# The gain row norm_g spread by TensorE instead of by a load, and the last row tile cut into 512, 384 and 128 columns

## The chip, the cores and the metric

The kernel runs on one core of one Trainium2 chip. The time is device microseconds of one execution; the figure for a kernel is the median over its runs. TensorE multiplies matrices, ScalarE (ACT in the profile), VectorE (DVE) and GpSimd (POOL) work on rows of up to 128 partitions, and SyncE (SP) issues most of the loads and stores. ScalarE can issue some as well.

## The reference, cut to what matters

One decoder block over 1,040 tokens of 1,024 features: 16 learned meta tokens stand ahead of 1,024 real ones.

```python
def rmsnorm(x, g):
    xf = x.astype(jnp.float32)
    xf = xf * lax.rsqrt(jnp.mean(xf * xf, axis=-1, keepdims=True) + RMS_EPS)
    return (xf * g.astype(jnp.float32)).astype(x.dtype)

def hybrid_layer(x, norm_g, w_in, ...):
    h = rmsnorm(x, norm_g)
    proj = jnp.einsum('bld,dn->bln', h, w_in)
    u_pool, z_pool, q, k, v, z_attn, f_logit, g_pool, g_attn = jnp.split(proj, ...)
    y_pool = causal_multiscale_pool(u_pool, pool_w, pool_scale) * jax.nn.silu(z_pool)
    y_attn = forgetting_attention(q, k, v, log_f).reshape(...) * jax.nn.silu(z_attn)
    merged = (jax.nn.sigmoid(g_pool) * jnp.einsum('blc,cd->bld', y_pool, w_up_pool)
              + jax.nn.sigmoid(g_attn) * jnp.einsum('blc,cd->bld', y_attn, w_up_attn))
    return x + jnp.einsum('bld,de->ble', merged, w_out)

h = rmsnorm(hybrid_layer(concat([meta, x]), ...), final_norm_g)[:, N_META:]
```

The change touches both ends: the first `rmsnorm` with the gain `norm_g`, and the last product with `w_out`, the residual sum and the final `rmsnorm`.

## The kernel before, in words

**Arithmetic.** Every fp32 factor is split into a high part in the fp32r format and the rest (`whi` and `wlo` of the weights, `hh` and `hl` of the normalized tokens). A product is three matmuls: high by high, low by high, high by low. A projection piece (`g_proj`, L139) has 8 blocks of 128 features and so 24 matmuls into one PSUM bank, `pj`.

**The start.** From L346 on, each engine does its work in the order in which it is written. The tokens come in nine tiles of 128 rows, `xt`. For each tile ScalarE squares it and sums the rows (`norm_scale`, L171), GpSimd adds EPS and takes the power -0.5 (`rstd_of`, L110 and L111), and VectorE multiplies the tile by that `rstd` and by the gain in one instruction (L174). For the gain it reads `gb`, the row `norm_g` in all 128 partitions; two loads of 256 KB put it there, which read the same 2 KB of the row 128 times each. TensorE then turns the scaled tile in two groups of four transposes (L185), ScalarE copies each group to `hh` (L187) and VectorE subtracts for `hl` (L188). ScalarE also makes the high part of each weight (L366). GpSimd subtracts for the low part (L371); for the q weight GpSimd takes one half and VectorE the other.

TensorE's order is: 12 warm-up matmuls on a tile of ones (`WARM`, L353, their result is not used), the transposes of tiles 0 and 1, the q piece of the first 256 tokens (the 16 meta tokens have no query, so it has 240 columns), the transposes of tile 2, the k piece, the transposes of tile 3, the v piece, and then the same for the next 256 tokens. A piece's result is copied from PSUM by ScalarE (`qa` at L211, `ka`, `vt`), so ScalarE does its later work only behind it. The v weight's high part stands on ScalarE behind the q piece's copies.

**The middle.** Sixteen units of attention, the pooling mixer, the up projections and the spilled gates follow; a filler puts projection pieces between the attention's matmuls. Their order is the same before and after the change, apart from where GpSimd's two memsets of `ql` and one mask stand in the start.

**The end.** `out_tile(i, parts)` makes one of 8 row tiles of the output. For each part of the columns TensorE does 24 matmuls (`o_mm`, L839), VectorE adds the residual row `xr` (L853), ScalarE squares and sums (L854), and VectorE multiplies by `fgb`, the gain of the final norm. GpSimd adds up the sums (L858) and takes the power (L860). Then VectorE scales the left half, ScalarE the right half (L864), and each half is stored, by SyncE's and by ScalarE's queue. The parts are two of 512 columns, and in the last row tile 512, 256 and 256.

Of the kernel before, what the change touches and what calls it, by code (L numbers as in the profile page):

```python
# [20 lines left out]
EPS = 1e-6  # L21
# [8 lines left out]
HALVES = ((0, 512), (512, 1024))  # L30
# [8 lines left out]
NRC = 2  # L39
REC0 = 2  # L40
EVAC = (((0, 1),), ((0,), (1,)))
WARM = 12


def r32(ap):
    return ap.bitcast(F32)
# [7 lines left out]
def tile_hybrid_block(ctx, tc, x, meta, norm_g, w_in, b_forget, pool_w, pool_scale,  # L54
                      w_up_pool, w_up_attn, w_out, final_g, out):
    nc = tc.nc
    x2 = x.rearrange("b s d -> (b s) d")
    o2 = out.rearrange("b s d -> (b s) d")
# [12 lines left out]
    sm = ctx.enter_context(tc.tile_pool(name="sm", bufs=2))  # L71
    dr = ctx.enter_context(tc.tile_pool(name="dr", bufs=1, space=bass.MemoryType.DRAM))
    pj = ctx.enter_context(tc.tile_pool(name="pj", bufs=PJ, space=PS))
# [8 lines left out]
    epsp = cst.tile([128, 1], F32, name="epsp")  # L82
# [24 lines left out]
    def rstd_of(ss):  # L107
        n = ss.shape[0]
        r = sm.tile([128, 1], F32, name="rstd", bufs=4)
        nc.gpsimd.tensor_scalar(r[:n], ss, EPS, None, op0=ALU.add)  # L110
        nc.gpsimd.tensor_tensor(r[:n], r[:n], epsp[:n], op=ALU.pow)  # L111
        return r

# [39 lines left out]
    ap_ = A.enter_context(tc.tile_pool(name="ap", bufs=1))  # L153

    gb = gp.tile([128, D], F32, name="gb", tag="g")
    junk = gp.tile([128, D], F32, name="junk", tag="g")

    def norm_load(i):
        c0 = i * 128
        n = min(128, L - c0)  # L160
        xt = ap_.tile([128, D], F32, name="xt", tag="s", bufs=6)
        if i == 0:
            nc.sync.dma_start(xt[NM:], x2[:128 - NM, :])
            nc.sync.dma_start(xt[:NM], meta)
        else:
            nc.sync.dma_start(xt[:n], x2[c0 - NM:c0 - NM + n, :])
        return xt

    def norm_scale(xt, n, parts=((0, D),)):
        ss = sm.tile([128, 1], F32, name="ss")  # L170
        nc.scalar.activation(junk[:n], xt[:n], AF.Square, scale=D ** -0.5, accum_out=ss[:n])  # L171
        r = rstd_of(ss[:n])
        for c0, c1 in parts:
            nc.vector.scalar_tensor_tensor(xt[:n, c0:c1], xt[:n, c0:c1], r[:n], gb[:n, c0:c1],  # L174
                                           op0=ALU.mult, op1=ALU.mult)

    def norm_t(i, xt, n):
        c0 = i * 128
# [14 lines left out]
    def rows(e):  # L193
        return slice(64 * e, 64 * e + 64), slice(64 - 64 * e, 128 - 64 * e)

    def alloc_q(p):
        for e in range(2):
            QA[p, e] = gp.tile([128, SEQ], F32R, name="qa", tag="g")
            QL[p, e] = gp.tile([128, SEQ], F32R, name="ql", tag="g")
            nc.gpsimd.memset(r32(QL[p, e])[rows(e)[1]], 0.0)  # L200

    def alloc_k(p):
        for e in range(2):
            KA[p, e] = gp.tile([128, L], F32R, name="ka", tag="g")
# [141 lines left out]
    SM.enter_context(tc.manual_schedule())  # L346
    onesr = cst.tile([128, 128], F32R, name="onesr")
    nc.vector.memset(r32(onesr), 1.0)
    nc.scalar.activation(junk[:1, :2], r32(onesr)[:1, :2], AF.Square)
    xts = {0: norm_load(0)}  # L350
    warm = psO.tile([128, 512], F32, name="po")
    for i in range(WARM):
        nc.tensor.matmul(warm, onesr, onesr[:, None, :].to_broadcast([128, 4, 128]), start=True, stop=True)  # L353
    xts[1] = norm_load(1)
    for c0, c1 in HALVES:
        nc.sync.dma_start(gb[:, c0:c1], bass.AP(tensor=norm_g.tensor, offset=norm_g.offset + c0,
                                                ap=[[0, 128], [1, c1 - c0]]))

    def load_raw(col, pool=None, tag="raw"):
        raw = (pool or wp).tile([128, KO, 128], F32, name="raw", tag=tag)  # L360
# [3 lines left out]
    def split_hi(raw, pool, tag):  # L364
        hi = pool.tile([128, KO, 128], F32R, name="whi", tag=tag)
        nc.scalar.activation(hi, raw, AF.Copy)  # L366
        return hi
# [5 lines left out]

    rq = load_raw(COL_Q)
    xts[2] = norm_load(2)
    rk = load_raw(COL_K)
    xts[3] = norm_load(3)
# [3 lines left out]
    def scale_(i):  # L381
        norm_scale(xts[i], ntok(i))

    norm_scale(xts[0], 128, HALVES)
    norm_scale(xts[1], 128, HALVES)
    alloc_q(0)
    alloc_k(0)
    norm_t(0, xts[0], 128)
    hq_ = split_hi(rq, wp, "wh")
# [3 lines left out]
    norm_t(1, xts[1], 128)  # L393
    nc.vector.tensor_tensor(lq_[:, KO // 2:], rq[:, KO // 2:], r32(hq_)[:, KO // 2:], op=ALU.subtract)
    wq = (hq_, lq_)
    norm_scale(xts[2], 128, HALVES)
    hk_ = split_hi(rk, wp, "wh")
    wk = split_lo(rk, hk_, wp, "wl")
# [4 lines left out]
    for n, (kind, t0, t1) in enumerate(todo):  # L403
# [11 lines left out]
        i = {0: 2, 1: 3, 3: 4, 4: 5, 6: 6, 7: 7, 8: 8}.get(n)  # L415
# [268 lines left out]
    def btile(name, dt=F32, tag="b"):  # L684
        return bp.tile([128, SEQ], dt, name=name, tag=tag, bufs=8 if tag == "y" else 5)
# [149 lines left out]
    def o_mm(ps, i, c0, c1, ks):  # L835
        r = slice(i * 128, (i + 1) * 128)
        for k in ks:
            for n, (a, b) in enumerate(((0, 0), (0, 1), (1, 0))):
                nc.tensor.matmul(ps[:, :c1 - c0], mg[k][a][:, r], wo[k][b][:, c0:c1], start=(k == 0 and n == 0),  # L839
                                 stop=(k == KO - 1 and n == 2))  # L840

    def out_tile(i, parts):
        r = slice(i * 128, (i + 1) * 128)
        xr = btile("xr", F32, "y")
        sq = btile("sq", F32, "y")
        nc.sync.dma_start(xr, x2[r, :])
        ss = sm.tile([128, 4], F32, name="sso")
        tot = sm.tile([128, 1], F32, name="sst")
        for n, (ps, c0, c1) in enumerate(parts):
            if ps is None:  # L850
                ps = bank()
                o_mm(ps, i, c0, c1, range(KO))
            nc.vector.tensor_tensor(xr[:, c0:c1], ps[:, :c1 - c0], xr[:, c0:c1], op=ALU.add)  # L853
            nc.scalar.activation(sq[:, c0:c1], xr[:, c0:c1], AF.Square, scale=D ** -0.5, accum_out=ss[:, n:n + 1])  # L854
            if n == 0:
                nc.gpsimd.tensor_scalar(tot, ss[:, :1], EPS, None, op0=ALU.add)
            else:
                nc.gpsimd.tensor_tensor(tot, tot, ss[:, n:n + 1], op=ALU.add)  # L858
            nc.vector.tensor_tensor(xr[:, c0:c1], xr[:, c0:c1], fgb[:, c0:c1], op=ALU.mult)
        nc.gpsimd.tensor_tensor(tot, tot, epsp, op=ALU.pow)  # L860
        (a0, a1), (b0, b1) = HALVES
        nc.vector.tensor_scalar(sq[:, a0:a1], xr[:, a0:a1], tot, None, op0=ALU.mult)
        nc.sync.dma_start(o2[r, a0:a1], sq[:, a0:a1])
        nc.scalar.activation(sq[:, b0:b1], xr[:, b0:b1], AF.Copy, scale=tot)  # L864
        nc.scalar.dma_start(o2[r, b0:b1], sq[:, b0:b1])

    first = [(i, c0, c1, bank()) for i in range(3) for c0, c1 in HALVES]
    for i, c0, c1, ps in first:
# [3 lines left out]
    for i in range(3):  # L872
        out_tile(i, [(ps, c0, c1) for i2, c0, c1, ps in first if i2 == i])
    for i in range(3, 8):
        parts = HALVES if i < 7 else ((0, 512), (512, 768), (768, 1024))
        out_tile(i, [(None, c0, c1) for c0, c1 in parts])


# [26 lines left out]
```

## Time and profile before

| | |
|---|---|
| median of 3 runs | 799.68 us (799.35 to 800.86) |
| the profiled execution | 797.71 us, of which 796.0 us are the span of the core |
| mean granted TensorE clock of it | 0.984 of full speed |
| TensorE matmuls busy | 768.6 us, 97% of the span |
| TensorE weight loads busy (they overlap the matmuls) | 655.2 us, 82% |
| VectorE busy | 469.1 us, 59% |
| ScalarE busy | 394.6 us, 50% |
| GpSimd busy | 302.8 us, 38% |

The span is the time from the first to the last instruction that the profile records; the execution's own time lies 1.7 us above it. Busy is an average over the whole span. The profiled execution is one of many, and lies 1.97 us below the median of the timed runs.

### The profile page before, as it was taken

What the parts mean: (1) busy time and instruction counts of PE and PEld (TensorE: products, weight loads), DVE (VectorE), ACT (ScalarE), POOL (GpSimd) and SP (SyncE); (2) the same over time, 40 slices, a digit from 0 to 9 for tenths busy, and PEclk for the clock granted to TensorE, in tenths of its full rate; (3) what the DMA queues carried; (4) which work ended last, traced back from release to release, by engine and by line L of the source; (5) the groups of instructions that cost most, each with busy time, mean ns of one, the idle gap of its engine ahead of it and who ended that gap; (6) DMA issues with size and microseconds to landing.
All of it is one profiled execution on the core that took longest, in us unless ns stands there. A gap on an engine that the chain in (4) does not pass through costs nothing.

```text
span 796.0 us, 10676 instructions
## 1 busy us (share of the span) xinstructions
PE 768.6 (97%) x3893; PEld 655.2 (82%) x3893; DVE 469.1 (59%) x767; ACT 394.6 (50%) x754; POOL 302.8 (38%) x243
## 2 busy tenths in 40 slices
PE   7999999999999999999998899999997999999996
PEld 6997899998898888898977778888884888888885
DVE  4843667557677575586699894571246456444232
ACT  5752466446576564575455554463335445232121
POOL 5520226325325343254262362262887122222111
PEclk7999999999999999999998999999998999999999
DMA  9311122221311312212305333335753555533331
GB/s 296 83 28 27 52 65 71 78 76 40 94 41 48 91 47 75 80 34 68 105 1 153 106 101 100 99 92 165 219 180 106 177 181 171 185 106 106 105 107 53
DMA packets 74116, 79.86 MB, mean 100 GB/s; under 512 B 5552, under 2 KB 56752, under 8 KB 74064
## 3 DMA queue, kind: packets, MB, share of 16 engines
q1 hardware_dynamic: 68096, 59.79, 24.7%
q10 hardware_dynamic: 5968, 19.40, 7.8%
q8 instruction: 30, 0.49, 0.3%
q14 instruction: 22, 0.18, 0.1%
HBM read 58.10 MB, written 21.07 MB: 99 GB/s over the span
## 4 chain that ended last, share of the span: by engine, by line
PE 85%; DVE 8%; issue 2%; DMA 2%; ACT 1%; POOL 1%; SPq 0%; POOLq 0%; DVEq 0%; ACTq 0%
PE pj L139 62%; PE pj L839 11%; PE po L590 4%; PE ps L525 2%; PE ps L524 2%; DVE s L752 1%; DVE pl L574 1%; DMA u<-sp_u 1%; PE pj L445 1%; DVE m L540 1%; DVE u L756 1%; DMA gb<-in_norm_g_dram 1%; PE pt L553 1%; DVE S L569 1%; PE pt L545 1%
## 5 line engine op out<-in xcount | busy, mean ns | idle before, releaser
L139 PE MATMUL pj<-hh,whi 128*128 128x512 f32 (+4 forms) x768 | 183.0, 365 | 1.4 <-DVE ql L215 0.9
L139 PE MATMUL pj<-hh,wlo 128*128 128x512 f32 (+4 forms) x768 | 183.2, 363 | 0.0
L128 POOL TENSOR_TENSOR wlo<-raw,whi 128x1024 fp32r<-128x1024 f32 x37 | 91.3, 2469 | 239.0 <-ACT whi L127 81.9
L139 PE MATMUL pj<-hl,whi 128*128 128x512 f32 (+4 forms) x768 | 178.1, 361 | 0.0
L139 PEld LDWEIGHTS pj<-hh,whi 128*128 128x128 f32 x768 | 132.7, 191 | 19.2 <-PE pj L249 1.1
L139 PEld LDWEIGHTS pj<-hh,wlo 128*128 128x128 f32 x768 | 133.1, 191 | 16.8
L139 PEld LDWEIGHTS pj<-hl,whi 128*128 128x128 f32 x768 | 132.3, 190 | 17.4 <-DVE hl L188 0.2
L574 DVE TENSOR_TENSOR pl<-S,ph 128x512 fp32r<-128x512 f32 (+4 forms) x112 | 84.4, 765 | 15.7 <-ACT ph L573 14.8
L582 POOL TENSOR_TENSOR acc<-acc,S 128x272 f32<-128x272 f32 (+4 forms) x80 | 79.0, 988 | 19.4 <-ACT S L570 10.4
L533 ACT ACTIVATE S<-ps,negc 128x400 f32<-128x400 f32 (+2 forms) x96 | 49.0, 515 | 55.9 <-DVE S L531 49.9
L540 DVE TENSOR_TENSOR m<-m,S 128x272 f32<-128x272 f32 (+4 forms) x80 | 55.1, 689 | 18.1 <-ACT S L533 16.7
L569 DVE TENSOR_TENSOR S<-S,pt 128x512 f32<-128x512 f32 (+4 forms) x112 | 50.2, 499 | 17.8 <-PE pt L553 17.7
L573 ACT ACTIVATE ph<-S 128x512 fp32r<-128x512 f32 (+4 forms) x112 | 52.5, 479 | 11.8 <-PE po L590 11.3
L570 ACT ACTIVATE S<-S 128x512 f32<-128x512 f32 (+4 forms) x112 | 48.1, 477 | 16.2 <-DVE S L569 16.1
L839 PE MATMUL pj<-wol,gh 128*128 128x512 f32 (+1 forms) x136 | 51.7, 380 | 0.0
L839 PE MATMUL pj<-woh,gl 128*128 128x512 f32 (+1 forms) x136 | 51.7, 380 | 0.0
L839 PE MATMUL pj<-woh,gh 128*128 128x512 f32 (+1 forms) x136 | 51.6, 379 | 0.0
L819 POOL TENSOR_TENSOR gl<-rl,gh 128x512 fp32r<-128x512 f32 x16 | 22.6, 1412 | 72.5 <-ACT gh L818 72.4
L127 ACT ACTIVATE whi<-raw 128x1024 fp32r<-128x1024 f32 x37 | 39.1, 1056 | 17.8 <-PE pj L139 17.6
L815 DVE TENSOR_TENSOR rl<-pj,rl 128x512 f32<-128x512 f32 x32 | 22.0, 690 | 40.1 <-PE pj L139 36.7
L287 ACT ACTIVATE st<-pj 128x512 f32<-128x512 f32 x48 | 28.5, 593 | 32.7 <-PE pj L139 23.4
L590 PE MATMUL po<-pl,V 128*128 128x512 f32 (+4 forms) x112 | 38.1, 340 | 2.8 <-DVE pl L574 2.8
(166 smaller groups left out, 1163.1 us busy)
## 6 DMA issues: line engine op xcount, KB each, us to landing
raw<-in_w_in_dram SPq DMA_DIRECT2D x40, 512.0 KB, 3.9
sp_gp<-st SPq DMA_DIRECT2D x16, 256.0 KB, 2.3
sp_ga<-st SPq DMA_DIRECT2D x16, 256.0 KB, 4.0
rl<-sp_gp ACTq DMA_DIRECT2D x8, 512.0 KB, 3.8
rl<-sp_ga ACTq DMA_DIRECT2D x8, 512.0 KB, 3.7
rawo<-in_w_out_dram SPq DMA_DIRECT2D x8, 512.0 KB, 4.0
xr<-in_x_dram SPq DMA_DIRECT2D x8, 512.0 KB, 3.8
xt<-in_x_dram SPq DMA_DIRECT2D x7, 512.0 KB, 9.4
```

The source lines that it names most:

```text
L127: nc.scalar.activation(hi, raw, AF.Copy)
L128: (eng or nc.gpsimd).tensor_tensor(lo, raw, r32(hi), op=ALU.subtract)
L139: nc.tensor.matmul(ps, a, b, start=(i == 0), stop=(i == len(seq) - 1))
L533: nc.scalar.activation(s[:kb, f0:], ps[:kb, f0:], AF.Identity, bias=nb_)
L540: nc.vector.tensor_tensor(m[:kb, c0:], m[:kb, c0:], s[:kb, c0:], op=ALU.max)
L569: dves.append(nc.vector.tensor_tensor(s[:kb, c0:], s[:kb, c0:], self.pm[:kb, c0:], op=ALU.subtract))
L570: exps.append(nc.scalar.activation(s[:kb, c0:], s[:kb, c0:], AF.Exp))
L573: nc.scalar.activation(ph[:kb, c0:], s[:kb, c0:], AF.Copy)
L574: nc.vector.tensor_tensor(pl[:kb, c0:], s[:kb, c0:], r32(ph[:kb, c0:]), op=ALU.subtract)
L582: nc.gpsimd.tensor_tensor(acc[:kb, c0:], acc[:kb, c0:], s[:kb, c0:], op=ALU.add)
L590: nc.tensor.matmul(self.po[:, c0:], v, r[:kb, c0:], start=(b == 0 and i == 0), stop=(b == self.nb - 1 and i == 1))
L839: nc.tensor.matmul(ps[:, :c1 - c0], mg[k][a][:, r], wo[k][b][:, c0:c1], start=(k == 0 and n == 0), stop=(k == KO - 1 and n == 2))
```

## The change

At the start, `norm_g` comes as one row of 4 KB into one partition, by ScalarE's queue. Two matmuls, with a row of ones as the stationary side, put the row into 128 partitions of two PSUM banks. They stand behind four warm-up matmuls, one more follows, and the other seven go. The scaling of tiles 0 and 1 reads the gain from PSUM. Behind tile 1, ScalarE copies both banks to `gb` for the later tiles. The 16 meta rows are loaded by ScalarE's queue instead of SyncE's, and VectorE adds EPS instead of GpSimd. GpSimd's memsets of `ql` come later.

At the end, the last row tile is cut at 512 and 896 instead of 512 and 768. In all row tiles the last of the sums is added by VectorE, with one instruction of one column, instead of GpSimd. In the last one VectorE scales and stores 640 columns and ScalarE 384.

```diff
@@ constants
-WARM = 12
+WARM = (4, 1)
+LAST = ((0, 512), (512, 896), (896, 1024))
@@ rstd_of
-        nc.gpsimd.tensor_scalar(r[:n], ss, EPS, None, op0=ALU.add)
+        nc.vector.tensor_scalar(r[:n], ss, EPS, None, op0=ALU.add)
@@ norm_load, tile 0
-            nc.sync.dma_start(xt[:NM], meta)
+            nc.scalar.dma_start(xt[:NM], meta)
@@ norm_scale
-            nc.vector.scalar_tensor_tensor(xt[:n, c0:c1], xt[:n, c0:c1], r[:n], gb[:n, c0:c1],
-                                           op0=ALU.mult, op1=ALU.mult)
+            g = gps[c0 // 512][:n] if gps else gb[:n, c0:c1]
+            nc.vector.scalar_tensor_tensor(xt[:n, c0:c1], xt[:n, c0:c1], r[:n], g, op0=ALU.mult, op1=ALU.mult)
@@ the start
+    grow = ap_.tile([1, D], F32, name="grow")
+    nc.scalar.dma_start(grow, norm_g)
...
+    warm_up(WARM[0])
+    gps = []
     for c0, c1 in HALVES:
-        nc.sync.dma_start(gb[:, c0:c1], bass.AP(tensor=norm_g.tensor, offset=norm_g.offset + c0,
-                                                ap=[[0, 128], [1, c1 - c0]]))
+        pg = pj.tile([128, 512], F32, name="pj")
+        nc.tensor.matmul(pg, r32(onesr)[:1], grow[:, c0:c1], start=True, stop=True)
+        gps.append(pg)
+    warm_up(WARM[1])
@@ behind norm_t(1) and the halves of the q weight's low part
+    for g, (c0, c1) in zip(gps, HALVES):
+        nc.scalar.activation(gb[:, c0:c1], g, AF.Copy)
+    gps.clear()
+    alloc_q(0)
     norm_scale(xts[2], 128, HALVES)
@@ out_tile
+            elif n < len(parts) - 1:
+                nc.gpsimd.tensor_tensor(tot[:, :1], tot[:, :1], ss[:, n:n + 1], op=ALU.add)
             else:
-                nc.gpsimd.tensor_tensor(tot, tot, ss[:, n:n + 1], op=ALU.add)
+                nc.vector.tensor_scalar(tot[:, 1:], ss[:, n:n + 1], tot[:, :1], None, op0=ALU.add)
+                nc.gpsimd.tensor_tensor(tot[:, 1:], tot[:, 1:], epsp, op=ALU.pow)
...
-        (a0, a1), (b0, b1) = HALVES
...
+        (a0, a1), (b0, b1) = HALVES if i < 7 else ((0, 640), (640, 1024))
```

ScalarE's order from the start of the program to the square of tile 2 was this before (`xt` is a token tile, `hh_115` and `hh_116` the two halves of `hh`, `whi` a weight's high part, `junk` a result that is not used):

```order
L349 ACT_TABLE_LOAD
L349 ACTIVATE junk<-onesr 1x2
L171 ACTIVATE junk,ss<-xt 128x1024 x2
L187 ACTIVATE hh_115<-pt 128x4x128
L187 ACTIVATE hh_116<-ps 128x4x128
L366 ACTIVATE whi<-raw 128x1024
L187 ACTIVATE hh_115<-pt 128x4x128
L187 ACTIVATE hh_116<-ps 128x4x128
L171 ACTIVATE junk,ss<-xt 128x1024
```

After the change the same stretch reads:

```order
L351 DMA grow<-in_norm_g_dram 1x1024
L165 DMA xt<-in_meta_tokens_dram 16x1024
L353 ACT_TABLE_LOAD
L353 ACTIVATE junk<-onesr 1x2
L172 ACTIVATE junk,ss<-xt 128x1024 x2
L188 ACTIVATE hh_115<-pt 128x4x128
L188 ACTIVATE hh_116<-ps 128x4x128
L376 ACTIVATE whi<-raw 128x1024
L188 ACTIVATE hh_115<-pt 128x4x128
L188 ACTIVATE hh_116<-ps 128x4x128
L406 ACTIVATE gb<-pj 128x512 x2
L172 ACTIVATE junk,ss<-xt 128x1024
```

Two loads are issued ahead of all work, and the two copies of `gb` from PSUM stand between the copies of tile 1 and the square of tile 2, with the splits and the later squares behind them.

VectorE's order from the scaling of tile 0 to that of tile 3 was this before (`hl` is the low part of the tokens, `wlo` the half of the q weight's low part):

```order
L174 SCALAR_TENSOR_TENSOR xt<-xt,rstd,gb 128x512 x4
L188 TENSOR_TENSOR hl_117<-pt,hh_115 128x4x128
L188 TENSOR_TENSOR hl_118<-ps,hh_116 128x4x128
L188 TENSOR_TENSOR hl_117<-pt,hh_115 128x4x128
L188 TENSOR_TENSOR hl_118<-ps,hh_116 128x4x128
L394 TENSOR_TENSOR wlo<-raw,whi 128x512
L174 SCALAR_TENSOR_TENSOR xt<-xt,rstd,gb 128x512 x2
L174 SCALAR_TENSOR_TENSOR xt<-xt,rstd,gb 128x1024
```

After the change the same stretch, to the EPS of tile 3, reads:

```order
L111 TENSOR_SCALAR rstd<-ss 128x1
L176 SCALAR_TENSOR_TENSOR xt<-xt,rstd,pj 128x512 x2
L111 TENSOR_SCALAR rstd<-ss 128x1
L176 SCALAR_TENSOR_TENSOR xt<-xt,rstd,pj 128x512 x2
L189 TENSOR_TENSOR hl_117<-pt,hh_115 128x4x128
L189 TENSOR_TENSOR hl_118<-ps,hh_116 128x4x128
L189 TENSOR_TENSOR hl_117<-pt,hh_115 128x4x128
L189 TENSOR_TENSOR hl_118<-ps,hh_116 128x4x128
L403 TENSOR_TENSOR wlo<-raw,whi 128x512
L111 TENSOR_SCALAR rstd<-ss 128x1
L176 SCALAR_TENSOR_TENSOR xt<-xt,rstd,gb 128x512 x2
L111 TENSOR_SCALAR rstd<-ss 128x1
```

The adds of EPS to the row sums stand between the scalings, so that of tile 1 comes behind both halves of tile 0. Tiles 0 and 1 are scaled by the PSUM banks `pj`, tile 2 and the later ones by `gb`.

## Rows read from the trace of the kernel before

**Rows 1.** Chain of waits, first 32 us (start us, us, what).
```profile
2.17 6.66 DMA gb<-in_norm_g_dram
...
13.85 5.43 PE pj L139 x24
20.76 2.82 PE pj L139 x24
24.46 6.02 PE pj L139 x48
```

**Rows 2.** Windows: stretch, us, busy of PE, PEld, DVE, ACT, POOL; granted clock, DMA, GB/s.
```profile
9.00:19.00 10.00, 8.83 (x40) 8.43 (x40) 8.39 (x10) 6.13 (x10) 7.64 (x8) 0.50 1.09 361
19.10:25.00 5.90, 5.66 (x48) 5.32 (x47) 4.18 (x7) 5.60 (x12) 4.24 (x5) 1.00 1.00 260
```

**Rows 3.** Timeline of the start (start us, us, what [idle before, released by]).
```profile
1.31 4.92 PE L353 MATMUL po<-onesr 128*128 128x512 f32 x12 [1.31 <-DVE car L477]
...
4.77 1.06 ACT L171 ACTIVATE junk<-xt 128x1024 f32<-128x1024 f32 x1 [2.48 <-DMA xt<-in_meta_tokens_dram]
...
6.46 0.57 POOL L111 TENSOR_TENSOR rstd<-rstd,epsp 128x1 f32<-128x1 f32 x1
...
7.54 1.06 ACT L171 ACTIVATE junk<-xt 128x1024 f32<-128x1024 f32 x1 [1.62 <-DMA xt<-in_x_dram]
...
8.95 2.74 DVE L174 SCALAR_TENSOR_TENSOR xt<-xt,rstd,gb 128x512 f32<-128x512 f32 x4 [7.68 <-DMA gb<-in_norm_g_dram]
...
9.76 1.12 PE L185 MATMUL pt<-ident,xt 128*128 128x128 f32 x4 [3.53 <-DVE xt L174]
```

**Rows 4.** Timeline of ScalarE, 13 to 22 us.
```profile
13.68 0.60 ACT L187 ACTIVATE hh<-ps 128x512 fp32r<-128x512 f32 x1
14.16 1.07 ACT L171 ACTIVATE junk<-xt 128x1024 f32<-128x1024 f32 x1
...
19.30 1.49 ACT L211 ACTIVATE qa<-pj 64x240 fp32r<-64x240 f32 x4 [2.01 <-PE pj L139]
20.70 1.05 ACT L366 ACTIVATE whi<-raw 128x1024 fp32r<-128x1024 f32 x1
```

**Rows 5.** Timelines of VectorE and GpSimd, 16 to 25 us.
```profile
16.41 2.37 POOL L371 TENSOR_TENSOR wlo<-raw,whi 128x1024 fp32r<-128x1024 f32 x1
16.48 3.51 DVE L174 SCALAR_TENSOR_TENSOR xt<-xt,rstd,gb 128x512 f32<-128x512 f32 x2 [0.77 <-POOL rstd L111]
...
19.49 0.93 POOL L111 TENSOR_TENSOR rstd<-rstd,epsp 128x1 f32<-128x1 f32 x1
...
20.45 1.29 DVE L174 SCALAR_TENSOR_TENSOR xt<-xt,rstd,gb 128x1024 f32<-128x1024 f32 x1 [0.47 <-POOL rstd L111]
...
21.83 2.42 POOL L371 TENSOR_TENSOR wlo<-raw,whi 128x1024 fp32r<-128x1024 f32 x1 [1.41 <-ACT whi L366]
```

**Rows 6.** Timeline of TensorE: the last 48 matmuls, the first and the last.
```profile
783.73 0.28 PE L839 MATMUL pj<-woh,gh 128*128 128x256 f32 x1
...
789.25 0.28 PE L839 MATMUL pj<-woh,gl 128*128 128x256 f32 x1
```

**Rows 7.** Timeline of TensorE's weight loads, 143.2 to 143.6 us.
```profile
143.28 0.19 PEld L139 LDWEIGHTS pj<-hh,wlo 128*128 128x128 f32 x1
...
143.39 0.19 PEld L590 LDWEIGHTS po<-ph,V 128*128 128x128 f32 x1
```

**Rows 8.** Timelines of VectorE, ScalarE and GpSimd after the last matmul.
```profile
789.57 0.42 DVE L853 TENSOR_TENSOR xr<-pj,xr 128x256 f32<-128x256 f32 x1 [1.39 <-PE pj L839]
...
790.03 0.42 ACT L854 ACTIVATE sq<-xr 128x256 f32<-128x256 f32 x1 [2.31 <-DVE xr L853]
...
790.68 0.36 POOL L858 TENSOR_TENSOR sst<-sst,sso 128x1 f32<-128x1 f32 x1 [2.45 <-ACT sq L854]
791.12 0.57 POOL L860 TENSOR_TENSOR sst<-sst,epsp 128x1 f32<-128x1 f32 x1
...
791.72 0.72 ACT L864 ACTIVATE sq<-xr,sst 128x512 f32<-128x512 f32 x1 [1.19 <-POOL sst L860]
```

More of the change, by code (lines that the diff above doesn't have):

```diff
@@ L348, in tile_hybrid_block, with warm_up @@
     nc.vector.memset(r32(onesr), 1.0)
+    grow = ap_.tile([1, D], F32, name="grow")
+    nc.scalar.dma_start(grow, norm_g)
+    xts = {0: norm_load(0)}
     nc.scalar.activation(junk[:1, :2], r32(onesr)[:1, :2], AF.Square)
-    xts = {0: norm_load(0)}
+    xts[1] = norm_load(1)
     warm = psO.tile([128, 512], F32, name="po")
-    for i in range(WARM):
-        nc.tensor.matmul(warm, onesr, onesr[:, None, :].to_broadcast([128, 4, 128]), start=True, stop=True)
-    xts[1] = norm_load(1)
+    def warm_up(n):
+        for i in range(n):
+            nc.tensor.matmul(warm, onesr, onesr[:, None, :].to_broadcast([128, 4, 128]), start=True, stop=True)
+    warm_up(WARM[0])
+    gps = []
     for c0, c1 in HALVES:
-        nc.sync.dma_start(gb[:, c0:c1], bass.AP(tensor=norm_g.tensor, offset=norm_g.offset + c0,
-                                                ap=[[0, 128], [1, c1 - c0]]))
+        pg = pj.tile([128, 512], F32, name="pj")
+        nc.tensor.matmul(pg, r32(onesr)[:1], grow[:, c0:c1], start=True, stop=True)
+        gps.append(pg)
+    warm_up(WARM[1])
     def load_raw(col, pool=None, tag="raw"):
@@ L385, in tile_hybrid_block @@
     norm_scale(xts[1], 128, HALVES)
-    alloc_q(0)
     alloc_k(0)
@@ L847, in out_tile @@
         ss = sm.tile([128, 4], F32, name="sso")
-        tot = sm.tile([128, 1], F32, name="sst")
+        tot = sm.tile([128, 2], F32, name="sst")
         for n, (ps, c0, c1) in enumerate(parts):
@@ L855, in out_tile @@
             if n == 0:
-                nc.gpsimd.tensor_scalar(tot, ss[:, :1], EPS, None, op0=ALU.add)
-            else:
-                nc.gpsimd.tensor_tensor(tot, tot, ss[:, n:n + 1], op=ALU.add)
+                nc.gpsimd.tensor_scalar(tot[:, :1], ss[:, :1], EPS, None, op0=ALU.add)
+            elif n < len(parts) - 1:
+                nc.gpsimd.tensor_tensor(tot[:, :1], tot[:, :1], ss[:, n:n + 1], op=ALU.add)
+            else:
+                nc.vector.tensor_scalar(tot[:, 1:], ss[:, n:n + 1], tot[:, :1], None, op0=ALU.add)
+                nc.gpsimd.tensor_tensor(tot[:, 1:], tot[:, 1:], epsp, op=ALU.pow)
             nc.vector.tensor_tensor(xr[:, c0:c1], xr[:, c0:c1], fgb[:, c0:c1], op=ALU.mult)
-        nc.gpsimd.tensor_tensor(tot, tot, epsp, op=ALU.pow)
-        (a0, a1), (b0, b1) = HALVES
-        nc.vector.tensor_scalar(sq[:, a0:a1], xr[:, a0:a1], tot, None, op0=ALU.mult)
+        (a0, a1), (b0, b1) = HALVES if i < 7 else ((0, 640), (640, 1024))
+        nc.scalar.activation(sq[:, b0:b1], xr[:, b0:b1], AF.Copy, scale=tot[:, 1:])
+        nc.scalar.dma_start(o2[r, b0:b1], sq[:, b0:b1])
+        nc.vector.tensor_scalar(sq[:, a0:a1], xr[:, a0:a1], tot[:, 1:], None, op0=ALU.mult)
         nc.sync.dma_start(o2[r, a0:a1], sq[:, a0:a1])
-        nc.scalar.activation(sq[:, b0:b1], xr[:, b0:b1], AF.Copy, scale=tot)
-        nc.scalar.dma_start(o2[r, b0:b1], sq[:, b0:b1])
     first = [(i, c0, c1, bank()) for i in range(3) for c0, c1 in HALVES]
@@ L874, in tile_hybrid_block @@
     for i in range(3, 8):
-        parts = HALVES if i < 7 else ((0, 512), (512, 768), (768, 1024))
+        parts = HALVES if i < 7 else LAST
         out_tile(i, [(None, c0, c1) for c0, c1 in parts])
```

## The prediction

> **What bounds the kernel now.** I read the chain of waits first, over the first 25 us: the reader is to see that it does not begin with arithmetic but with a load, the 128-fold copy of norm_g, from 2.17 to 8.83, and that TensorE then carries it: the q piece of 24 matmuls from 13.85 to 19.28, the k piece from 20.76 to 23.58 [rows 1]. Then the windows with the granted clock: 0.50 from 9 to 19 us, that is 1.2 GHz, and 1.00 (2.4 GHz) from 19.1 on [rows 2], so the clock rises just before the k piece. Then the timeline of the start [rows 3], of ScalarE [rows 4], and of VectorE against GpSimd [rows 5], because the places between those two TensorE stretches are set there. Last the tail [rows 6 to 8]. Order is the same in between, so what is gained by the v piece, and what is lost on the last row tile, is all that the change can do directly.
>
> **The change part by part: the start.**
>
> *The load.* The scaling of row tile 0 sat idle for norm_g until 8.95, although its rstd was done at 6.46 + 0.57 = 7.03 [rows 3]. With the load gone, the scaling starts at about 7.0: 1.9 us earlier. (The add of EPS moves from GpSimd to VectorE; that may give some tenths more, and I count nothing.)
>
> *Is the spread there in time?* Four warm-up matmuls end at 1.31 + 4 x 0.41 = 2.95 (12 of them take 4.92) [rows 3]. The 4 KB row is issued at about the time of the first x load, and that load and the meta rows, 512 KB in all, had landed at 4.77 [rows 3]; the row lands no later. No matmul of this kind is in the trace: a pass of 512 columns costs 0.41 as in the warm-up; four passes, my upper bound, 1.64. The halves are then ready at 6.4 and 8.05 at the latest, at 3.8 and 4.2 at the earliest if the row lands at 3.4. They are needed at 7.0 and 7.7. Cost: 0, at worst 0.4; I take 0, the work of tile 0's square and rstd covers it.
>
> *Tile 1.* Its square is released by its own load at 7.54 [rows 3], which I leave there. 7.54 + 1.06, the read of the sum (about 0.2), the add, now on VectorE behind tile 0's scalings, and 0.57 for the power give 9.6; it was 8.95 + 2 x 0.69 = 10.3. One half scaled (0.69), four transposes at half clock (1.12) and one ScalarE copy (0.60) [rows 3, 4] put the q piece at about 12.0 instead of 13.85: 1.85 earlier.
>
> *The copies of gb.* Two ScalarE copies of 128x512 from PSUM come between tile 1's copies and the square of tile 2. The step from such a copy to the next instruction is 14.16 - 13.68 = 0.48 [rows 4], so 0.96 in all. The square of tile 2, the split of the k weight and everything behind them on ScalarE are then earlier by 0.9 only.
>
> *Where that 0.9 goes.* The scaling of tile 2 and GpSimd's subtract for the k weight started together, at 16.48 and 16.41; the scaling took 3.51 for two halves that take 1.37 at the start (2.74 for four) [rows 3, 5]: 2.1 us lost to the 2.37 us subtract. Both hang on the same ScalarE stretch, both move by 0.9 and meet again. The k piece stands on TensorE behind tile 2's transposes, so it starts at 20.76 - 0.9 = 19.9.
>
> *The clock in the k piece.* The q piece ends by 12.0 + 5.43 = 17.4. TensorE then waits some 2 us, with four transposes in it. Before, it had worked on from 13.85 with no such pause and got the full clock at 19.1. After its other pause, from 6.23 (1.31 + 4.92) to 9.76, it stood at 1.2 GHz [rows 2, 3]. If the k piece runs at half clock it costs 2.82 more, if at full clock nothing. I take 1.0, part of the piece, nearer to the row that shows a pause followed by half clock but with a shorter pause. End of the k piece: 23.58 - 0.9 + 1.0 = 23.7.
>
> *Tile 3.* Here the earlier q piece triggers a new collision. Before, tile 3 was scaled from 20.45 to 21.74 while GpSimd stood idle until 21.83 for the split of the v weight, which ScalarE could only make at 20.70 because it had waited 2.01 us for the q piece [rows 4, 5]. With q done at 17.4 or earlier, that split ends at 19.85 or earlier; tile 3's power ends at 20.42 - 0.9 = 19.5, and GpSimd goes straight into the 2.42 us subtract, as it did at 16.41. The scaling ends at about 19.6 + 2.4 + 1.29 = 23.3 instead of 21.74. Its transposes followed the k piece at 23.58 anyway, so this loss hides behind that of the clock: the v piece follows the later of 23.7 and 23.3, against 23.58. If the clock holds, 23.3 is the bound and 0.3 is gained.
>
> Start, sum: 0.0 (-0.3 to +0.1 as worked). Bounds: -1.85 when nothing behind the q piece binds, +1.9 when the whole k piece runs at half clock.
>
> **The last row tile.** Before, the 48 matmuls of 256 columns start every (789.25 - 783.73) / 47 = 0.1175 [rows 6]. 24 of 384 columns, by columns, start every 0.176: 4.2 us. For 128 columns half of 0.1175 would be 0.059, 1.4 us, and TensorE would end when it did. But each matmul loads its own weights, and where short matmuls follow each other the loads start at 143.28 and 143.39 [rows 7], 0.11 apart: 24 x 0.11 = 2.6 us. I take that, since it is the row of the very limit: 4.2 + 2.6 - 5.6 = **+1.2** (bounds 0 and 1.2).
>
> The Trainium skill (TensorE: Matmul & The Clock Gate, Back-to-back issue gap) gives about 81 ns per matmul of 128 columns in a stream with its weight loads. By that the piece would take 24 x 0.081 = 1.9 and TensorE would end 0.5 later, not 1.2. The row of this trace is slower than that page.
>
> What follows the last matmul took 789.57 to 791.72 + 0.72 = 792.44, that is 2.87 [rows 8]. The add of 0.42 and the square of 0.42 work on half the columns: I take 0.1 off each. GpSimd's add with its hand-over, 791.12 - 790.68 = 0.44, becomes a VectorE add of one column, about 0.15: 0.3 off. The last copy has 384 instead of 512 columns: 0.72 x 0.25, 0.15 off. The read, the power (0.57) and the store stay, and VectorE's 640 columns run beside ScalarE's 384. Sum **-0.65** (-0.4 to -0.9). The last tile: +0.55, bounds -0.9 and +0.8. The same VectorE add in tiles 0 to 6 is hidden: TensorE's matmuls run on, and the add stands before a multiply that waits for the same square.
>
> **Sum.** 0.0 + 0.55 = +0.5 on the profiled execution's 797.71 (span 796.0 and 1.7 around it): 798.2. The median of the runs is 1.97 above it. I put that down to the clock: in the profiled execution it rose just as the k piece began, the best case; a run in which it rises later pays in the k piece already before the change, and the 1.0 that I charged above is then no new loss. On the median the sum is so between -0.5 and +0.5; I take -0.2: **799.5**.
>
> **The rivals.**
>
> *Faster: the start's gain survives.* If VectorE is first at tile 3, or the v weight arrives late, and the clock stays up, the k piece's 0.9 reaches the v piece; if the copies of gb do not bind either, 1.85 does. With a last tile at its lower bound of -0.9: 799.7 - 0.9 - 0.9 = 797.9, to 799.7 - 1.85 - 0.9 = 796.9. For it: the long idle time ahead of the scaling, which truly goes. Against it: the 3.51 us scaling [rows 5], which shows that VectorE does wait out GpSimd.
>
> *Slower: the pause costs the clock.* If TensorE's pause ahead of the k piece leaves it at 1.2 GHz for the whole of the k piece and part of the v piece, 2.8 to 3.3 are lost against 0.9 gained; with +0.55 at the end 799.7 + 2.5 to 3.0 = 802.2 to 802.7. It decides once more than about 4 us of matmuls run at half clock after 19.9. For it: the pause at 6.23 and the 10 us at half clock that followed. Against it: the median already holds executions with a later rise, and the transposes of tile 2 break the pause.
>
> *The change does not do what it says* (the spread is late, the scaling waits as long as before): the k piece starts where it did and the tail adds 0.55: 800.2, within my forecast's band.
>
> **How the numbers follow.** About 0.2%, 1.6 us, is what a measurement of this kernel can tell from no change. My forecast, no change by that measure, with the spread-is-late rival inside it: 0.60. Faster rival: 0.27. Slower rival: 0.13. The likeliest case gives 799.5, its own range 798.1 to 801.2. Leaving out a tenth at each end of all cases gives 797.2 to 801.5.
>
> **What would show it right or wrong.** In the changed profile: the first scaling at about 7.0; the q piece at about 12.0; the k piece at 19 to 20 and the v piece within 0.5 us of 24.46; a scaling of tile 3 of over 3 us beside a GpSimd subtract; half clock in or near the k piece; loads of weights 0.11 apart in the last 128 columns, and some 2.2 us from the last matmul to the last copy's end. I am wrong if the scaling of tile 3 takes 1.3 us and the v piece starts before 23.5, or if the 128 columns take about 1.4 us: then it is the faster rival.

## The result and the profile after

The changed kernel takes 801.35 us, median of 18 runs (800.1 to 801.91); the kernel before takes 799.77 in the runs beside it. The ratio is 1.0017, 95% interval 1.0011 to 1.0024: slower by 1.4 us (0.9 to 1.9). Forecast were 799.5 and a range of 797.2 to 801.5. The time lies in the range, but outside the likeliest case's own (798.1 to 801.2), and a slight gain was forecast where there is a loss. The loss is smaller than the 0.2% that the prediction took for no change, but 18 runs tell it from none.

The profiled execution after has a time of 800.97 us and a span of 799.2. The timeline of its start (start us, us, what, idle before and its releaser) answers to [rows 3 to 5]:

```profile
3.32 3.78 PE L365 MATMUL pj<-grow,onesr 1*128 1x512 f32 x4
...
5.77 1.06 ACT L172 ACTIVATE junk<-xt 128x1024 f32<-128x1024 f32 x1 [2.55 <-DMA xt<-in_meta_tokens_dram]
...
7.18 0.56 POOL L112 TENSOR_TENSOR rstd<-rstd,epsp 128x1 f32<-128x1 f32 x1 [5.29 <-DVE rstd L111]
...
7.78 1.40 DVE L176 SCALAR_TENSOR_TENSOR xt<-xt,rstd,pj 128x512 f32<-128x512 f32 x2 [0.68 <-POOL rstd L112]
...
12.66 1.35 PE L140 MATMUL pj<-hh,whi 128*128 128x240 f32 x8
...
13.14 1.08 ACT L406 ACTIVATE gb<-pj 128x512 f32<-128x512 f32 x2
...
14.09 1.07 ACT L172 ACTIVATE junk<-xt 128x1024 f32<-128x1024 f32 x1
...
16.18 3.51 DVE L176 SCALAR_TENSOR_TENSOR xt<-xt,rstd,gb 128x512 f32<-128x512 f32 x2 [0.74 <-POOL rstd L112]
16.28 2.86 POOL L381 TENSOR_TENSOR wlo<-raw,whi 128x1024 fp32r<-128x1024 f32 x1
17.03 0.63 PE L186 MATMUL pt<-ident,xt 128*128 128x128 f32 x4 [1.22 <-issue]
...
19.84 1.09 PE L186 MATMUL ps<-ident,xt 128*128 128x128 f32 x4 [2.18 <-DVE rstd L111]
20.36 2.39 POOL L381 TENSOR_TENSOR wlo<-raw,whi 128x1024 fp32r<-128x1024 f32 x1
20.42 3.40 DVE L176 SCALAR_TENSOR_TENSOR xt<-xt,rstd,gb 128x1024 f32<-128x1024 f32 x1 [0.67 <-POOL rstd L112]
...
20.57 2.06 PE L140 MATMUL pj<-hh,whi 128*128 128x256 f32 x8
...
25.21 1.19 PE L140 MATMUL pj<-hh,whi 128*128 128x256 f32 x8
...
29.54 1.34 PE L140 MATMUL pj<-hl,whi 128*128 128x256 f32 x8 [0.33 <-DVE hl L189]
```

The wait for norm_g is gone, and the q piece starts 1.2 us earlier. Then the gain runs out. The second half of tile 2's scaling waits out GpSimd's subtract, TensorE stands between the two groups of tile 2's transposes, and the k piece starts at 20.57, where it started before (20.52), but on half clock. The scaling of tile 3 waits out the next subtract. The v piece starts at 25.21, after 24.21 before, and ahead of 29.54 TensorE waits 0.33 for tile 3's low part on VectorE.

The windows with the granted clock (columns as in [rows 2]) show full clock for the q piece and 0.68 for the k piece; before, the clock was 0.50 and 1.00 there:

```profile
12.60:16.10 3.50, 3.16 (x25) 2.84 (x24) 2.08 (x4) 3.46 (x8) 3.29 (x4) 1.00 1.08 378
19.80:24.30 4.50, 4.46 (x27) 4.49 (x28) 3.87 (x3) 2.01 (x4) 2.91 (x2) 0.68 0.96 236
```

The end answers to [rows 6, 8]: first and last matmul of the last two parts, then what follows the last one.

```profile
786.18 0.34 PE L852 MATMUL pj<-woh,gh 128*128 128x384 f32 x1
...
790.40 0.22 PE L852 MATMUL pj<-woh,gh 128*128 128x128 f32 x1
...
792.91 0.28 PE L852 MATMUL pj<-woh,gl 128*128 128x128 f32 x1
793.23 0.29 DVE L866 TENSOR_TENSOR xr<-pj,xr 128x128 f32<-128x128 f32 x1 [0.83 <-PE pj L852]
...
794.06 0.21 DVE L873 TENSOR_SCALAR sst<-sso,sst 128x1 f32<-128x1 f32 x1 [0.54 <-ACT sq L867]
...
794.35 0.57 POOL L874 TENSOR_TENSOR sst<-sst,epsp 128x1 f32<-128x1 f32 x1 [1.90 <-DVE sst L873]
794.95 0.62 ACT L877 ACTIVATE sq<-xr,sst 128x384 f32<-128x384 f32 x1 [1.00 <-POOL sst L874]
```

The 24 matmuls of 128 columns are (792.91 - 790.40) / 23 = 0.109 us apart. From the first to the last of the 48 it is 6.73 us after 5.52: **+1.21**. From the last matmul's start to the end of the last copy it is 795.57 - 792.91 = 2.66, after 792.44 - 789.25 = 3.19: **-0.53**.

Three marks show where the rest of the 3.2 us between the two spans arose. ScalarE's first copy of a gate piece to `st` started at 102.25 before and at 102.95 after: in these two executions the start costs 0.70. TensorE's last eight matmuls on the tokens (`hh,wlo`) started 0.92 later, and VectorE's last products of the up projections (`rl`) 2.12:

```profile
102.25 0.49 ACT L297 ACTIVATE st<-pj 128x384 f32<-128x384 f32 x1
...
597.93 2.02 PE L139 MATMUL pj<-hh,wlo 128*128 128x512 f32 x8
...
702.56 1.28 DVE L815 TENSOR_TENSOR rl<-pj,rl 128x512 f32<-128x512 f32 x2
```

```profile
102.95 0.49 ACT L298 ACTIVATE st<-pj 128x384 f32<-128x384 f32 x1
...
598.85 2.02 PE L140 MATMUL pj<-hh,wlo 128*128 128x512 f32 x8
...
704.68 1.28 DVE L828 TENSOR_TENSOR rl<-pj,rl 128x512 f32<-128x512 f32 x2
```

So 1.42 us arose between the first mark and the last, where the program is the same, and 1.20 of it behind the second. The granted clock falls twice between the first and the last in both executions. From 410 to 430 us it was lower before (0.83) than after (0.91), and the changed kernel lies less than 1 us behind on either side of it. Around 606 us it was low for longer after. The windows there of before, of after and of the third experiment (t3, which has the unchanged start) in this order:

```profile
596.00:626.00 30.00, 24.32 (x93) 18.06 (x92) 18.60 (x19) 15.29 (x19) 15.32 (x7) 0.89 0.44 148
```

```profile
596.00:626.00 30.00, 24.64 (x88) 18.29 (x87) 18.05 (x18) 14.49 (x18) 15.32 (x7) 0.83 0.42 137
```

```profile
596.00:626.00 30.00, 23.69 (x84) 17.49 (x84) 17.85 (x16) 14.30 (x19) 14.47 (x7) 0.83 0.39 131
```

The 0.06 over 30 us are 1.8 us of full clock. The third row has the start of before and the low value all the same; of the 14 profiled executions of this study 11 had 0.83 there, and of the three with 0.89 one has the start of before and two (u1, u2) have changed ones. Between the second mark and the last, t1 and t3, both with the unchanged start, took 0.8 and 2.0 us longer than the profile of before, the changed kernel 1.2. So this part is luck of the execution from which the prediction was made, and not the change: what the runs charge to the change is 1.4 us, not 3.2. (Another 0.3 of the 3.2 arose in the row tiles ahead of the last; t2, with the old `out_tile`, has it too.)

### The profile page after: what moved, and what is told of

Same layout as the page of the kernel before. It is cut to its first block, busy times and chain, and to the rows that moved or that the text cites. A ratio compares the mean times of both kernels' runs of the same rounds, so it can differ in the third digit from the quotient of the medians.

```text
span 799.2 us, 10670 instructions
## 1 busy us (share of the span) xinstructions
PE 771.7 (97%) x3890; PEld 654.7 (82%) x3890; DVE 471.5 (59%) x784; ACT 395.4 (49%) x756; POOL 295.5 (37%) x226
## 4 chain that ended last, share of the span: by engine, by line
PE 82%; DVE 9%; issue 3%; ACT 2%; DMA 2%; POOL 1%; POOLq 0%; SPq 0%; DVEq 0%; ACTq 0%
PE pj L140 59%; PE pj L852 11%; PE po L603 4%; PE ps L538 2%; PE ps L537 2%; DVE s L765 1%; DVE pl L587 1%; DMA u<-sp_u 1%; PE pj L458 1%; DVE S L582 1%; DVE m L553 1%; PE pt L566 1%; DVE u L769 1%; PE pt L558 1%; DMA raw<-in_w_in_dram 1%
## 5 line engine op out<-in xcount | busy, mean ns | idle before, releaser
L595 POOL TENSOR_TENSOR acc<-acc,S 128x272 f32<-128x272 f32 (+4 forms) x80 | 79.0, 988 | 19.4 <-ACT S L583 10.4
L852 PE MATMUL pj<-wol,gh 128*128 128x512 f32 (+2 forms) x136 | 52.2, 384 | 0.0
L852 PE MATMUL pj<-woh,gl 128*128 128x512 f32 (+2 forms) x136 | 52.1, 383 | 0.0
L852 PE MATMUL pj<-woh,gh 128*128 128x512 f32 (+2 forms) x136 | 52.1, 383 | 0.0
```

Of the source, the lines that this page charges most:

```text
L595: nc.gpsimd.tensor_tensor(acc[:kb, c0:], acc[:kb, c0:], s[:kb, c0:], op=ALU.add)
```

## The experiments

Each time is a ratio to the kernel before in the same job; microseconds are that ratio times 799.7.

**t1 and t2: each end alone.** t1 is the kernel before with the new `out_tile` and cut, t2 the changed kernel with the old ones. The edit of t1, beside the lines of `out_tile` that the change's diff shows:

```diff
-        parts = HALVES if i < 7 else ((0, 512), (512, 768), (768, 1024))
+        parts = HALVES if i < 7 else LAST
```

> The kernel before with the changed out_tile and the last tile in 512, 384 and 128 columns; the start is untouched. Theory A (two separate losses, one at each end): the last 48 matmuls end 1.2 us later, the chain behind them is 0.5 shorter, so the time is 0.7 us above before (+0.5 to +0.9) and the middle is as before. Rival B (the start alone is to blame, the end pays for itself): within 0.2 us of before. Rival C (the profiled run of after shows a low clock for 3.4 us more in the up projections, and that belongs to the change): no difference here but the 0.7 at the end, the rest in the next kernel.

> The changed start with the old out_tile. Theory A: the start costs 0.7 to 0.9 us: the scaling of tile 3 takes 3.4 us beside GpSimd's subtract, the k piece starts on half clock, and the drift against before that is there at 42 us (about +0.7) is still there at the last tile. Rival B: 1.6 us. Rival C: drift at 42 us below 0.3, and the loss comes with the low clock around 606 us.

t1: 1.0011 (1.0002 to 1.0021), +0.9 us. t2: 1.0008 (0.9999 to 1.0018), +0.6 us. Together 1.5, as the whole change. In t1's trace the last 48 matmuls and what follows them take as long as in the changed kernel. Theory A stands and B falls, by little: t1's interval begins at 0.2 us, and t2's ends at 1.4. C falls by t1, which also had 0.83 from 596 to 626 us, with the start of before.

**t3: the new code of the out tiles without the new cut.** t1 without the edit above: the kernel before with the new `out_tile`, the last tile in 512, 256 and 256.

> The kernel before with the changed out_tile, but the last tile still in 512, 256 and 256 columns. Theory A: TensorE ends as before, the chain behind the last matmul is shorter by the moved add and the smaller copy alone, 0.4 us: time 0.4 below before (-0.2 to -0.6). Rival D (the code of the out tiles, not the cut, costs the time at the end): +0.3 or more.

1.0003 (0.9992 to 1.0014): no difference. The interval alone does not exclude rival D, but the trace shows the end shorter, not longer. The timeline from its last matmul on shows why the hoped 0.4 did not come:

```profile
793.19 0.42 DVE L853 TENSOR_TENSOR xr<-pj,xr 128x256 f32<-128x256 f32 x1 [1.39 <-PE pj L839]
...
794.26 0.21 DVE L860 TENSOR_SCALAR sst<-sso,sst 128x1 f32<-128x1 f32 x1 [0.65 <-ACT sq L854]
794.39 0.41 DVE L862 TENSOR_TENSOR xr<-xr,fgb 128x256 f32<-128x256 f32 x1
794.55 0.68 POOL L861 TENSOR_TENSOR sst<-sst,epsp 128x1 f32<-128x1 f32 x1 [2.71 <-DVE sst L860]
795.26 0.61 ACT L864 ACTIVATE sq<-xr,sst 128x384 f32<-128x384 f32 x1 [1.11 <-POOL sst L861]
```

From VectorE's add to the end of the last copy it takes 2.68, before 2.87 [rows 8]: 0.19 less, 0.11 of it in the copy. The add of the sums left GpSimd, but the power starts 0.29 after it, and takes 0.68 beside VectorE's product instead of 0.57. Most of the 0.53 of the full change thus comes from the short last part, which costs TensorE 1.21.

The same run is the best look at the unchanged start in another execution. Its clock was low from about 10.4 to 13.8 only, not from 9 to 19 as in [rows 2], so that the q piece had full clock and ended early; TensorE then stood until tile 2 came at 19.53, and the k piece fell on half clock:

```profile
14.00:17.00 3.00, 2.96 (x24) 2.77 (x24) 2.23 (x4) 3.00 (x5) 2.25 (x4) 1.00 1.09 352
20.80:23.80 3.00, 3.00 (x16) 3.00 (x16) 3.00 (x1) 1.63 (x3) 2.92 (x2) 0.50 0.89 222
```

Its v piece started at 25.88, 1.7 us later than in the profile that the prediction was made from. Tile 3's scaling took 3.40 there, beside a subtract that started 0.07 ahead of it at 20.49: with an early q piece the unchanged kernel meets the second collision too.

**t4 and u1: no collision.** In t4 tiles 2 and 3 too read the gain from PSUM (one bank is `po`, which is free there, so that the k piece finds a `pj` bank), and ScalarE's copies to `gb` come behind tile 2's. In u1 the copies stay ahead of tile 2's square.

```diff
-        pg = pj.tile([128, 512], F32, name="pj")
+        pg = psO.tile([128, 512], F32, name="po") if c0 else pj.tile([128, 512], F32, name="pj")
...
-    scale_(3)
+    norm_scale(xts[3], 128, HALVES)
...
             last_n = norm_t(i, xts[i], ntok(i))
+            if n == 0:
+                for g, (c0, c1) in zip(gps, HALVES):
+                    nc.scalar.activation(gb[:, c0:c1], g, AF.Copy)
+                gps.clear()
```

> The changed kernel, but tiles 2 and 3 too read the gain from PSUM, and ScalarE copies it to gb only behind tile 2's copies. Theory A (VectorE waits out GpSimd because it reads tile and gain from the same memory that GpSimd reads): both scalings take about 1.4 us beside the same subtract, the k piece starts at 17 to 18 us instead of 20.6, on full clock, the v piece 2 to 4 us earlier than in after, and the time falls by 1 to 2.5 us against after: 0 to 1 us below before. Rival E (the scaling is slow for another reason, such as the weight loads' traffic into the same memory): the scalings still take 3.4 us, and only the 1 us of ScalarE's copies is gained in the place of tile 2's square; time as after.

> As t4 (tiles 2 and 3 scaled by the gain in PSUM), but ScalarE's two copies to gb stand where the change put them, ahead of the square of tile 2. It parts the two things that t4 took away. Theory A (the collision of the scaling with GpSimd's subtract is what ate the gain): scalings of 0.75 us per half as in t4, v piece within 0.5 us of t4's 21.8, time within 0.4 us of t4. Rival F (the 1 us of copies on ScalarE's path is worth as much): v piece at 22.8 or later and the time 1 us above t4.

t4: 0.9974 (0.9962 to 0.9986), -2.1 us, which is 3.4 us below the changed kernel, where theory A had 1 to 2.5. u1: 0.9980 (0.9969 to 0.9990). The timeline of t4:

```profile
16.13 2.35 POOL L382 TENSOR_TENSOR wlo<-raw,whi 128x1024 fp32r<-128x1024 f32 x1
16.19 0.75 DVE L176 SCALAR_TENSOR_TENSOR xt<-xt,rstd,pj 128x512 f32<-128x512 f32 x1 [1.34 <-POOL rstd L112]
...
16.85 0.74 DVE L176 SCALAR_TENSOR_TENSOR xt<-xt,rstd,po 128x512 f32<-128x512 f32 x1
...
18.12 1.19 PE L140 MATMUL pj<-hh,whi 128*128 128x256 f32 x8
...
21.82 1.18 PE L140 MATMUL pj<-hh,whi 128*128 128x256 f32 x8
```

The subtract started first, as in the kernel before, and VectorE ran at its full pace beside it: 0.75 a half instead of 3.51 for two. The k piece came 2.4 us earlier than before and the v piece 2.4 earlier, on full clock. Rivals E and F fall: what ate the gain is the collision, and the copies are worth nothing that a run can tell.

**w1 and w2: one collision each.** As u1, with only tile 3 (w1) or only tile 2 (w2) reading PSUM besides tiles 0 and 1. The edit of w2 (`norm_scale` takes `gps` as an argument now; w1 has it the other way round):

```diff
-    norm_scale(xts[2], 128, HALVES)
-    norm_scale(xts[3], 128, HALVES)
+    norm_scale(xts[2], 128, HALVES, gps)
+    scale_(3)
```

> As u1, but only tile 3 (with tiles 0 and 1) reads the gain from PSUM; tile 2 reads gb again. Theory A, as the prediction had it (tile 3's collision is covered by the k piece, which starts late and on half clock because of tile 2's collision): tile 2's scaling 3.5 us, the k piece starts at 20.5 at half clock and the v piece at 25.2 as in after; what remains to gain is the stall of 0.5 us ahead of the low-part pass of the second q piece: 0 to 0.7 us below after. Rival J (tile 3's collision alone makes the loss): v piece at 23.5, 2 us or more below after.

> As u1, but only tile 2 (with tiles 0 and 1) reads the gain from PSUM; tile 3 reads gb and meets GpSimd's subtract for the v weight. Theory A: k piece at 18.2 on full clock, its end at 21; tile 3's scaling takes 3.4 us, from 19.3 to 22.7, and is now bare: v piece at 23.4 to 23.7, 1.5 to 1.8 us earlier than in after; time 1.2 to 1.8 us below after. Rival J: v piece no earlier than 24.5, less than 0.7 us gained.

w1: 1.0003 (0.9994 to 1.0011). In its profile the k piece ran wholly on half clock (2.06, 1.91 and 1.91 us for its three passes) and the v piece waited for it until 26.61: tile 3's collision alone does not decide, as theory A had it, and J falls. The time, 1.1 us below the changed kernel, is a little more than expected; the profiled execution, 801.16 us, is w1's slowest, so its trace does not show where that was gained. w2: 0.9976 (0.9967 to 0.9985), nearly all of what t4 gained, and 3.3 us below the changed kernel where theory A had 1.2 to 1.8. Its GpSimd and VectorE at tile 3 (two timelines):

```profile
19.45 0.56 POOL L112 TENSOR_TENSOR rstd<-rstd,epsp 128x1 f32<-128x1 f32 x1
20.48 3.15 POOL L382 TENSOR_TENSOR wlo<-raw,whi 128x1024 fp32r<-128x1024 f32 x1 [0.47 <-ACT whi L377]
```

```profile
20.04 1.28 DVE L176 SCALAR_TENSOR_TENSOR xt<-xt,rstd,gb 128x1024 f32<-128x1024 f32 x1 [1.56 <-POOL rstd L112]
```

Here I had expected a scaling of 3.4 us. But VectorE started first, took its usual 1.28, and GpSimd waited: 3.15 instead of 2.4. The v piece started at 22.65. So w2 does not show what a slow scaling of tile 3 costs by itself. The Trainium skill (SBUF — State Buffer, SBUF: two separate sides) calls the port pair that the two engines share an exclusive lock, which an instruction that starts first holds to its end, and names VectorE's instructions with two inputs in SBUF among those that need it against a GpSimd instruction that reads there. These traces agree: 3.51 or 3.40 with `gb`, 0.75 with PSUM, and the loser changes with the order of the starts.

**u2: hold the clock.** Seven more matmuls on the tile of ones stand ahead of each half of tile 2's transposes.

```diff
         for j in range(2):
+            if fill:
+                fill(7)
...
-            last_n = norm_t(i, xts[i], ntok(i))
+            last_n = norm_t(i, xts[i], ntok(i), warm_up if n == 0 else None)
```

> The changed kernel with 7 more warm-up matmuls ahead of each half of tile 2's transposes, in the pause between the q and the k piece; results unused. If they keep the granted clock at 1.00 there, the k piece takes 2.8 us instead of 3.8. Theory A (tile 3's late scaling is right behind the clock): the v piece starts only 0.3 to 0.5 us earlier than in after, at 24.7 to 24.9, and the time falls by no more than 0.5 us. Rival G (the low clock in the k piece is the loss of the start): v piece at 24.2, time 1 us below after.

1.0054 (1.0037 to 1.0071), +4.3 us. The clock did stay up, and the passes of the k piece took 1.19, 1.10 and 1.10. The v piece still started at 25.22, and neither at A's 24.7 to 24.9 nor at G's 24.2, because tile 3's scaling (20.80 to 24.25) now ended last. That much answers theory A's question: with the clock up, the other collision is next. The +4.3 says nothing on it: the scheduler that orders ScalarE's work behind this place put two more squares ahead of the k piece's copies, the second of which did not start until 26.46, so that the copies came at 27.52 (24.62 in the changed kernel). So the price of the low clock by itself was not measured apart.

**w3 and w4: undo one part.** The meta rows by SyncE again (w3); EPS by GpSimd again (w4).

```diff
-            nc.scalar.dma_start(xt[:NM], meta)
+            nc.sync.dma_start(xt[:NM], meta)
```

> The changed kernel with one part undone: the 16 meta rows are loaded by SyncE's queue, ahead of tile 1. Theory A: tile 0 is complete at 4.8 instead of 5.8, its scaling starts at 6.9 instead of 7.8, the q piece at 11.8; but tile 2's scaling still collides, 0.9 us earlier, so the v piece is 0.5 to 0.9 us earlier and the time 0.4 to 0.9 us below after. Rival K (a longer pause of TensorE, more of the k piece at half clock): v piece within 0.2 us of after, time as after.

> The changed kernel with another part undone: GpSimd adds EPS again. In after the EPS of tile 4 stands on VectorE behind the slow scaling of tile 3 and was added at 25.80 (24.33 before). Theory L (the moved add passes VectorE's delay on to tile 4 and is part of the loss): tile 4's power at 24.5 or earlier, no stall ahead of the low-part pass of the second q piece, 0.3 to 0.8 us below after. Rival M (its place makes no difference): within 0.3 us of after.

w3: 1.0007 (0.9998 to 1.0015), 0.8 us below the changed kernel, as theory A had it and K did not, though the two intervals overlap. The scaling started at 6.77, the k piece, on full clock, at 19.74; tile 3's transposes then waited 0.71 for its scaling, and the v piece started at 24.34. w4: 1.0042 (1.0029 to 1.0055), 2 us above the changed kernel. Theory L falls, and M too. Its trace shows GpSimd starting first at tile 2:

```profile
16.67 2.35 POOL L381 TENSOR_TENSOR wlo<-raw,whi 128x1024 fp32r<-128x1024 f32 x1
```

```profile
16.73 3.49 DVE L176 SCALAR_TENSOR_TENSOR xt<-xt,rstd,gb 128x512 f32<-128x512 f32 x2 [1.96 <-POOL rstd L112]
```

In the changed kernel VectorE was 0.10 ahead, and its first half was through before it had to wait (the transposes started at 17.03; in w4 at 19.67). The k piece then ran on half clock for most of its length (passes of 2.06, 1.91 and 1.54 us). By 102 us w4 is 1.8 us behind the changed kernel. So VectorE's add of EPS is no loss: with it VectorE comes first at tile 2. The 1.8 us account for the 2 us within what the runs can tell.

**u4: what a short matmul costs.** The last tile in 512, 448 and 64 columns.

```diff
-LAST = ((0, 512), (512, 896), (896, 1024))
+LAST = ((0, 512), (512, 960), (960, 1024))
```

> The changed kernel with the last tile in 512, 448 and 64 columns. Theory A (each short matmul waits for its own weight load, 0.11 us): the last 24 matmuls start 0.109 to 0.112 us apart at 64 columns as at 128. Rival I (the pitch has a part that goes with the columns): 0.08 us or less.

Its one run took 802.02 us. The timeline of TensorE's weight loads, two of those between short matmuls, 20 steps apart:

```profile
791.61 0.19 PEld L852 LDWEIGHTS pj<-wol,gh 128*128 128x128 f32 x1
...
793.84 0.19 PEld L852 LDWEIGHTS pj<-woh,gh 128*128 128x128 f32 x1
```

The 20 steps take 2.23 us, 0.11 each, and at 128 columns it was 0.109: rival I falls, and the pitch (the time from one start to the next) goes with the load, not the columns. The Trainium skill (TensorE: Matmul & The Clock Gate, Back-to-back issue gap) gives about 81 ns at 128 columns; this kernel does not reach it.

**u3: the parts that pay.** t4 with the meta rows by SyncE and the last tile in 512, 256 and 256.

```diff
-            nc.scalar.dma_start(xt[:NM], meta)
+            nc.sync.dma_start(xt[:NM], meta)
...
-        parts = HALVES if i < 7 else LAST
+        parts = HALVES if i < 7 else ((0, 512), (512, 768), (768, 1024))
```

> t4 with the last tile in 512, 256 and 256 columns, and the 16 meta rows loaded again by SyncE's queue ahead of tile 1. Theory A: 0.7 us less than t4 by the cut, and up to 0.9 us less because tile 0 is complete and scaled at 7.0 instead of 7.8: 796.2 to 797.1, 2.6 to 3.5 us below before. Rival H (the start is now bound by the weights and GpSimd, not by tile 0): only the cut counts, 797.1 to 797.5.

0.9954 (0.9941 to 0.9968): 3.7 us faster than the kernel before and 5.0 faster than the changed one. Its first mark is at 98.44 us instead of t4's 99.49, and its time is 1.6 us below t4's, more than the cut's share (0.7, t1 against t3). So H falls: tile 0's 1 us does reach the end, once nothing collides.

## Why the prediction was wrong

- **The step that failed is the last one of the sum**, from +0.5 on the profiled execution to -0.2 on the median: "the 1.0 that I charged above is then no new loss". I put the 1.97 us between that execution and the median down to the clock in the k piece alone. The two other profiled executions with the unchanged start show otherwise. Up to the first mark t1 lies 0.2 us behind the profile of before and t3 1.5, and from there to the last mark each loses 2.2 us more, where the clock is low in the middle. That luck is the same for both kernels, and should not have been set against a loss of the change. With the +0.5 left to stand the forecast would have been 800.2: still short of the 1.4 measured, but on the right side.
- **The start was charged 0.0; t2 measured +0.6 (-0.1 to 1.4).** The load: right, the wait is gone. The scaling came at 7.78, not 7.0: tile 0's square was released by the meta rows at 5.77 instead of 4.77. I had taken the landing of the x load over unchanged for a transfer that was moved to another queue, behind the row and beside tile 1's load; w3 prices that at 0.8 us. The spread took four passes from 3.32 to 7.10, 0.9 us each instead of my 0.41, and was hidden as I said. The square of tile 2 came 0.07 earlier instead of 0.9. Taken with the step above, the forecast has the start at -0.7 on the median, 1.3 below t2: by w3 0.8 of that is the landing, and the rest the step. The runs' intervals do not part the two more sharply.
- **The two collisions were right**, down to 3.51 and 3.40 us, and so was the half clock in the k piece (bounds 0 and 2.8, 1.0 taken; from its start to the next transposes it is 24.42 - 20.57 = 3.85 us in this profile, after 23.42 - 20.52 = 2.90). TensorE's wait ahead of 29.54 was not seen, but it is no part of their price: t4, where nothing collides, has 0.32 us of it ahead of 26.15.
- **The last row tile was right in its terms.** TensorE: +1.2 forecast, +1.21 measured, by the row of the weight loads and not by the page. The work behind it: -0.65 forecast, -0.53 measured; the moved add gave less. In all +0.55 forecast, +0.68 in the trace, +0.9 (0.2 to 1.7) in t1.
- **The rivals.** The faster one named its condition rightly: without the waits behind GpSimd the gain survives (t4). The slower one's mechanism, a pause that brings the k piece to half clock, is what happened, at a third of its price.

## What to carry to other kernels

A wait that is taken away moves the work behind it: before it is booked as a gain, look which two engines then meet, and whether one can read its operand from PSUM instead. Here a gain kept in PSUM for two tiles longer turned a loss of 1.4 us into a gain of 2.1. Matmuls that load their own weights gain nothing below the column count at which the load sets the pitch (here 0.11 us at 64 and at 128 columns, 0.1175 at 256). And before a profiled execution's lead over the median is booked to one place, look in other executions where it arises.

## What the runs showed of the hardware

- Which of two instructions starts first decides who pays: VectorE ahead by 0.44 us at 20.04 took 1.28 us and GpSimd 3.15 (w2); GpSimd ahead by 0.06 us at 16.67 took 2.35 and VectorE 3.49 (w4).
- Spreading a row by a matmul of one-partition fp32 operands takes two passes of about 0.9 us per 512 columns (3.32 to 7.10 us in the changed kernel), while a warm-up matmul of 512 columns takes 0.41 (1.31 to 6.23 before).
- One stretch of low clock, around 606 us, in which TensorE is busy for 24 of 30 us, made 0.8 and 2.0 us of difference between executions in which the program of that stretch is the same (t1 and t3 against before).
